# State-space recurrence of a two-layer trunk: scan instructions in a rotating frame, with tables in another tile and the output products at another place on TensorE

## The chip, the cores and the metric

The kernel runs on one core of a Trainium2 chip. The metric is the device time of one execution in microseconds. Engines are named as in the profile: PE is TensorE, DVE is VectorE, ACT is ScalarE, POOL is GpSimd, SP is the queue that issues most DMAs.

## What is computed

A decoder trunk of two layers on 512 tokens of width 1024. Layer 0 projects the normed input once (q, k, v, gate of a retention head group and u of a state-space group), runs retention and the state-space mixer in parallel, joins them in one output projection, and goes through a mixture of 16 experts; layer 1 is dilated attention and a second mixture. The change touches the state-space mixer of layer 0, 32 groups of 16 channels with 64 complex states each:

```python
def s5_mixer(u, a_re, a_im, b_re, b_im, c_re, c_im, d_skip, log_dt, w_glu, b_glu):
    ...
    zr, zi = a_re * dt, a_im * dt
    mag = jnp.exp(zr)
    lam_re, lam_im = mag * jnp.cos(zi), mag * jnp.sin(zi)
    ...
    bu_re = jnp.einsum('blgh,gph->blgp', uf, bb_re)
    bu_im = jnp.einsum('blgh,gph->blgp', uf, bb_im)
    ...
    _, _, xr, xim = lax.associative_scan(combine, (ar, ai, bu_re, bu_im), axis=1)   # x[l] = lam * x[l-1] + bu[l]
    y = (jnp.einsum('blgp,ghp->blgh', xr, c_re.astype(f32))
         - jnp.einsum('blgp,ghp->blgh', xim, c_im.astype(f32))
         + d_skip.astype(f32) * uf)
    g = jax.nn.gelu(y.reshape(B, L, S5_WIDTH))
    return g * jax.nn.sigmoid(g @ w_glu.astype(f32) + b_glu.astype(f32))
```

## The kernel before

Everything is float32. A GEMM (`gemm`) runs as three products of 512 columns for each 128 rows of K (`mm3`, lines 197 to 199), from a high and a low part of each operand; `split_to` (line 194) makes the high part on ACT (a cast) and the low part on DVE (a product row "L194 TENSOR_TENSOR"), into a ring of three R tiles. A projection of 512 outputs takes 8 blocks of K, 4 token blocks and 3 products each: 96 products of `mm3`, in the order of K, and each token block is handed to an evacuation function at the end.

The state-space mixer works on chunks of 8 tokens, 64 of them, and in two halves `hf` of 16 groups. `s5_tables` makes the powers of lambda: `L` (0 to 8) and `M8` (lambda to the 8th, 16th, up to the 64th) by `cmul`, a complex product of six small DVE instructions. `s5_in_tables`, `s5_CL` and `s5_K` make the matrices for PE, on DVE, POOL, ACT and PE together. `s5_conv` computes what a chunk gives to itself, into the PSUM tiles `py`. `s5_in` gives each chunk's contribution X to the state (512 values for each of the real and the imaginary part of a half), `s5_scan` turns X into the states at the chunk ends, and `s5_cross` (line 598) adds C times the state before each chunk into `py`: 256 products of 32 by 63 in a half, followed by GELU on ACT.

`s5_scan` before does the recurrence over 64 chunk values as 8 blocks of 8: seven steps within all blocks, seven across the blocks' last values, seven that spread them. A step is four DVE instructions (lines 519 to 522), so 84 in a half.

`layer0_mix` calls, in this order: the v GEMM, the u GEMM, the tables, `s5_conv` of half 0, `s5_in` of both halves, the q GEMM, `s5_scan` and `s5_cross` of half 0, `s5_conv` of half 1, the k GEMM, `s5_scan` and `s5_cross` of half 1, then the gate GEMM, the GLU GEMM and the retention. `ev_q` and `ev_k` rotate q and k (`rot`: three DVE products, a POOL sum) and transpose them on PE (line 190). A scheduler orders each engine's instructions when the program is built, by program order and by when it expects operands; `tc.issue_after(x)` keeps what follows behind x on that engine. At run time each engine takes its instructions strictly in this order and waits at the first whose operands aren't there.

`growt` is the row tile of the norm weights; before, the next norm's row is loaded into it early on ACT's queue. `M8` shares its place with `srt`, a small table of the router. `m4s` are two work tiles of 1024 values, `spare4` holds `Bb` and `CTc`, tables that are read until `s5_CL` is done.

## Time and profile before

| | us |
|---|---|
| median of 3 runs | 1160.1 (1155.97 to 1160.4) |
| the profiled execution | 1166.1 |
| its span, first to last instruction | 1164.3 |
| PE busy in the span | 1061.4 (91%) |
| DVE busy in the span | 739.4 (64%) |

The profile is of one execution. Starts are counted from the span's beginning. A row's bracket tells how long its engine sat idle before it and which instruction ended that. PE's products are pipelined: two that follow each other start closer together than one of them is long, so steps between starts are used for what a run of them costs. [...]

### The profile page before, as it was taken

How to read it: one execution, taken by the hardware profiler on the slowest of the kernel's cores; microseconds unless marked ns; L12 is line 12 of the kernel's file. 1: busy time of each engine (PE TensorE's matmuls, PEld its weight loads, DVE VectorE, ACT ScalarE, POOL GpSimd, SP SyncE). 2: the span in 40 equal slices, each digit the busy share in tenths (PEclk: the TensorE clock that was granted, in tenths of full speed). 3: DMA queues.
4: the chain of work that ended last, by engine and by line, in shares of the span. 5: the costliest groups of instructions: out<-in, count | busy, mean ns of one | idle time of the engine just before them, and what ended most of it. 6: DMA issues, size and time to landing. Idle time of an engine off the chain costs nothing. (4 is left out here: it accounts for less than half of the span.)

```text
span 1164.3 us, 16088 instructions
## 1 busy us (share of the span) xinstructions
PE 1061.4 (91%) x5951; PEld 772.1 (66%) x5951; DVE 739.4 (64%) x1356; ACT 564.9 (49%) x853; POOL 188.2 (16%) x120
## 2 busy tenths in 40 slices
PE   6989877899789999999979999999978999999994
PEld 5767666787566765666448877877766676566641
DVE  6964957577687866756373264266578786666644
ACT  6333133614466755646352255254446675555634
POOL 3553120000121322111100000000012131211111
PEclk9999988999899999998989999999989999989998
DMA  8243032348398999999953223323439999999963
GB/s 252 74 144 110 36 113 74 110 153 312 107 399 334 383 397 375 388 365 359 334 205 110 90 73 145 109 73 141 191 130 402 347 387 396 384 387 370 367 257 145
DMA packets 84714, 277.39 MB, mean 238 GB/s; under 512 B 23715, under 2 KB 23899, under 8 KB 68369
## 3 DMA queue, kind: packets, MB, share of 16 engines
q1 hardware_dynamic: 72000, 248.31, 56.5%
q0 software_dynamic: 8016, 16.88, 5.8%
q10 hardware_dynamic: 4608, 11.06, 2.5%
q8 instruction: 51, 0.84, 0.3%
q14 instruction: 39, 0.31, 0.1%
HBM read 262.49 MB, written 24.12 MB: 246 GB/s over the span
## 5 line engine op out<-in xcount | busy, mean ns | idle before, releaser
L198 PE MATMUL acc<-R,R 128*128 128x512 f32 x936 | 384.4, 411 | 16.7 <-DVE R L194 15.9
L197 PE MATMUL acc<-R,R 128*128 128x512 f32 x860 | 354.1, 413 | 26.6 <-ACT R L194 16.5
L199 PE MATMUL acc<-R,R 128*128 128x512 f32 x860 | 345.2, 404 | 0.2 <-DVE R L194 0.2
L194 DVE TENSOR_TENSOR R<-F,R 128x1024 fp32r<-128x1024 f32 (+1 forms) x178 | 213.0, 1218 | 148.5 <-ACT R L194 144.3
L194 ACT CAST R<-F 128x1024 fp32r<-128x1024 f32 (+1 forms) x178 | 182.4, 1040 | 187.4 <-PE acc L199 115.4
L198 PEld LDWEIGHTS acc<-R,R 128*128 128x128 f32 x936 | 180.8, 193 | 66.8 <-DVE R L194 28.3
L197 PEld LDWEIGHTS acc<-R,R 128*128 128x128 f32 x860 | 166.1, 193 | 68.9 <-ACT R L194 22.9
L199 PEld LDWEIGHTS acc<-R,R 128*128 128x128 f32 x860 | 166.6, 194 | 36.3 <-DVE R L194 1.8
L1203 POOL DMA_INDIRECT F<-xnd,idx x30 | 51.0, 1700 | 238.0 <-DVE ws L1013 114.0
L1285 PE MATMUL acc<-F,R 128*64 128x512 f32 x304 | 71.2, 595 | 0.0
L194 DVE TENSOR_TENSOR R<-pb,R 128x512 fp32r<-128x512 f32 x84 | 56.7, 686 | 15.2 <-ACT R L194 15.2
L1357 POOL DMA_INDIRECT hd<-m,idx x20 | 36.6, 1832 | 152.1 <-ACT m L1356 130.2
L194 ACT CAST R<-pb 128x512 fp32r<-128x512 f32 x84 | 47.7, 587 | 27.1 <-PE pb L190 21.1
L903 POOL MEMSET R<- 128x1024 f32 x2 | 1.9, 955 | 313.2 <-PE acc L199 313.2
L194 DVE TENSOR_TENSOR R<-R,R 128x1024 fp32r<-128x1024 f32 x40 | 48.2, 1221 | 6.3 <-ACT R L194 5.9
L1285 PEld LDWEIGHTS acc<-F,R 128*64 128x64 f32 x304 | 22.0, 137 | 43.6 <-issue 42.6
L194 ACT CAST R<-R 128x1024 fp32r<-128x1024 f32 x40 | 41.3, 1050 | 13.5 <-PE acc L199 13.3
L197 PE MATMUL acc<-spare,R 128*128 128x512 f32 x116 | 46.0, 397 | 0.0
L199 PE MATMUL acc<-spare,R 128*128 128x512 f32 x116 | 45.9, 395 | 0.0
L190 PE MATMUL pb<-C,F 128*128 128x128 f32 (+1 forms) x296 | 38.3, 265 | 3.4 <-POOL F L478 3.4
L1288 ACT ACTIVATE m2w<-acc 64x512 f32<-64x512 f32 x8 | 4.8, 594 | 69.4 <-PE acc L1285 69.4
L190 PEld LDWEIGHTS pb<-C,F 128*128 128x128 f32 (+1 forms) x296 | 30.0, 142 | 10.9 <-issue 5.6
(379 smaller groups left out, 1464.7 us busy)
## 6 DMA issues: line engine op xcount, KB each, us to landing
F<-in_moe_w_up_dram SPq DMA_DIRECT2D x46, 1024.0 KB, 22.9
F<-in_moe_w_down_dram SPq DMA_DIRECT2D x40, 1024.0 KB, 22.1
F<-in_moe_w_gate_dram SPq DMA_DIRECT2D x38, 1024.0 KB, 22.8
R<-in_moe_w_gate_dram SPq DMA_DIRECT2D x20, 1024.0 KB, 23.6
R<-in_moe_w_down_dram SPq DMA_DIRECT2D x12, 1024.0 KB, 25.0
h<-in_moe_w_down_dram SPq DMA_DIRECT2D x12, 1024.0 KB, 22.2
F<-in_c_w_qkv_dram SPq DMA_DIRECT2D x12, 1024.0 KB, 5.7
F<-in_ab_w_in_dram SPq DMA_DIRECT2D x10, 1024.0 KB, 5.1
```

Source lines behind the costliest of these rows:

```text
L190: PE.transpose(dst, src, ident[:n, :n])
L194: return S.copy(hi, src), eng.tensor_tensor(lo, src, hi.bitcast(F32), op=OP.subtract)
L197: PE.matmul(ps, ah, bh, start=first, stop=False)
L198: PE.matmul(ps, ah, bl, start=False, stop=False)
L199: return PE.matmul(ps, al, bh, start=False, stop=last)
L903: G.memset(q.x0, 0.0)
L1203: rows[e] = G.indirect_dma_start(out=xg[e % 2][0:n], out_offset=None, in_=xnd[:, :], in_offset=bass.IndirectOffsetOnAxis(ap=idx[0:n, e, 0: ...
L1285: m = PE.matmul(ps[LIGHT * i:LIGHT * i + LIGHT], x_[:, 4 * kk + k, :], raw[i][:, k, :], start=kk + k == 0, stop=kk + k == 4, skip_group_ch ...
L1288: silu = S.activation(hs[0:LIGHT], ps[LIGHT:2 * LIGHT], AF.Silu)
L1357: G.indirect_dma_start(out=hd[:, :], out_offset=bass.IndirectOffsetOnAxis(ap=idx[:, e, 1:2], axis=0), in_=y[:, :], in_offset=None, bounds_ ...
```

## The change

The recurrence x[n] = r e^(i a) x[n-1] + b[n] (r and a are the modulus and the angle of lambda to the 8th) is done in a frame that turns by a at each step: with z[n] = e^(-i a n) x[n] it becomes z[n] = r z[n-1] + e^(-i a n) b[n], with a real factor, so the real and the imaginary part can each be done by one scan instruction over 8 rows of 64 values (`tensor_tensor_scan`; the factor is zero at each row's first value). `s5_tables` makes r (`r8`, an exponential on ACT) and the turning factors' powers 0 to 7 and 0, 8, up to 56 (`rot`, nine `cmul` instead of three for `M8`), in `growt`. A new function `s5_rotor` multiplies these out to 64 factors for each state (`E`, six DVE products of 512) and spreads r (`rt`, a copy and a memset); it uses an `m4s` tile and a part of `spare4`. `s5_scan` turns X (four products), scans it (two), and turns it back (four products): 10 instructions and the rotor's 8 for 84. The cross products are kept (`gemm.last`, which `gemm` now notes) behind the last product of the q GEMM (half 0) and of the k GEMM (half 1), the second rotor behind the last rotation of q. `srt` gets a place of its own.

```diff
...
@@ -394,7 +396,8 @@
         V.tensor_scalar(cs, cs, -2.0, 1.0, op0=OP.mult, op1=OP.add)
         L = F[H0][:, 896:1184].rearrange("p (a i q) -> p a i q", a=9, i=2)
         cmt = F[H0][:, 1184:1312].rearrange("p (i a q) -> p i a q", i=2, a=4)
-        M8 = sm.tile([128, 384], F32, bufs=1, tag="M8", name="M8").rearrange("p (m i q) -> p m i q", m=8, i=3)
+
+        r8, rot = growt[:, 544:560], growt[:, 0:544].rearrange("p (n i q) -> p n i q", n=17, i=2)
...
@@ -437,12 +440,21 @@
         V.tensor_tensor(t3[:, 1], Br[:, 0], cib, op=OP.mult)
         V.tensor_tensor(Bb[:, 0], Bb[:, 0], t3[:, 0], op=OP.subtract)
         V.tensor_tensor(Bb[:, 1], Bb[:, 1], t3[:, 1], op=OP.add)
-        N8 = M8[:, :, 0:3:2, :]
-        V.tensor_copy(N8[:, 0], L[:, 8])
-        cmul(N8[:, 1:2], N8[:, 0:1], N8[:, 0], 1)
-        cmul(N8[:, 2:4], N8[:, 0:2], N8[:, 1], 2)
-        cmul(N8[:, 4:8], N8[:, 0:4], N8[:, 3], 4)
-        V.tensor_scalar(M8[:, :, 1, :], M8[:, :, 2, :], -1.0, None, op0=OP.mult)
+        S.activation(r8, zr, AF.Exp, scale=8.0)
+        V.tensor_copy(rot[:, 1, 0, :], cs)
+        V.tensor_copy(rot[:, 1, 1, :], sn)
+        for i in (2, 3):
+            cmul(rot[:, i:i + 1], rot[:, i - 1:i], rot[:, i - 1], 1)
+        cmul(rot[:, 1:2], rot[:, 3:4], rot[:, 3], 1)
+        for g in (0, 9):
+            V.memset(rot[:, g, 0, :], 1.0)
+            V.memset(rot[:, g, 1, :], 0.0)
+            if g:
+                V.tensor_copy(rot[:, 10], rot[:, 8])
+            cmul(rot[:, g + 2:g + 3], rot[:, g + 1:g + 2], rot[:, g + 1], 1)
+            cmul(rot[:, g + 3:g + 5], rot[:, g + 1:g + 3], rot[:, g + 2], 2)
+            n = 3 if g else 4
+            cmul(rot[:, g + 5:g + 5 + n], rot[:, g + 1:g + 1 + n], rot[:, g + 4], n)
         bd = F[H1].rearrange("p (x i q t h) -> p x i q t h", x=2, i=2, q=16, t=2)
         CTd, Bbd = bd[:, 0], bd[:, 1]
         CTc = shaped(spare4[:, 512:1024], [128, 2, 16, 16])
@@ -457,7 +469,7 @@
                 S.copy(CTc[ps_, i], pc[ps_, :, two, :])
                 G.tensor_scalar(CTd[ps_, i, :, two, :], CTc[ps_, i], 1.0 - 2 * i, None, op0=OP.mult)
                 G.tensor_copy(Bbd[ps_, i, :, two, :], Bb[ps_, i])
-        P.update(L=L, M8=M8, Bb=Bb, CTc=CTc, CTd=CTd, Bbd=Bbd)
+        P.update(L=L, rot=rot, r8=r8, Bb=Bb, CTc=CTc, CTd=CTd, Bbd=Bbd)
         return P
 
     def s5_in_tables(P, hf, wslot):
@@ -499,34 +511,36 @@
             S.copy(X[:, i, 8 * hf:8 * hf + 8, :], px)
         return ins
 
-    def s5_scan(P, hf, X):
-        M8 = P["M8"]
+    def s5_rotor(P, hf):
+
         pr = slice(8 * hf, 8 * hf + 8)
-        B = X[:, :, pr, :].rearrange("p r q (b i) -> p r q b i", i=8)
-
-        def swap(v):
-
-            dims = [list(d) for d in v.ap]
-            return bass.AP(tensor=v.tensor, offset=v.offset + dims[1][0], ap=[dims[0], [-dims[1][0], 2]] + dims[2:])
-
-        def step(dst, src, m, n):
-
-            sh = [128, 2, 8, n]
-            mr = M8[:, m, 0, pr][:, None, :, None].to_broadcast(sh)
-            mi = M8[:, m, 1:3, pr][:, :, :, None].to_broadcast(sh)
-            ta = m2([128, 2, 8, 8], "sca")[:, :, :, 0:n]
-            tb = m2([128, 2, 8, 8], "scb")[:, :, :, 0:n]
-            V.tensor_tensor(ta, src, mr, op=OP.mult)
-            V.tensor_tensor(tb, swap(src), mi, op=OP.mult)
-            V.tensor_tensor(dst, dst, ta, op=OP.add)
-            V.tensor_tensor(dst, dst, tb, op=OP.add)
-
-        for i in range(1, 8):
-            step(B[:, :, :, :, i], B[:, :, :, :, i - 1], 0, 8)
-        for b in range(1, 8):
-            step(B[:, :, :, b, 7:8], B[:, :, :, b - 1, 7:8], 7, 1)
-        for i in range(7):
-            step(B[:, :, :, 1:8, i], B[:, :, :, 0:7, 7], i, 7)
+        E = shaped(m4s[hf], [128, 2, 512])
+        rt = shaped(spare4[:, 512 * hf:512 * hf + 512], [128, 8, 64])
+        sh = [128, 8, 8, 8]
+        b_ = [P["rot"][:, 0:8, i, pr].rearrange("p n q -> p q n")[:, :, None, :].to_broadcast(sh) for i in range(2)]
+        a_ = [P["rot"][:, 9:17, i, pr].rearrange("p n q -> p q n")[:, :, :, None].to_broadcast(sh) for i in range(2)]
+        e = [shaped(E[:, i], sh) for i in range(2)]
+        t = shaped(m4s[1 - hf][:, 0:512], sh)
+        for i in range(2):
+            V.tensor_tensor(e[i], a_[0], b_[i], op=OP.mult)
+            V.tensor_tensor(t, a_[1], b_[1 - i], op=OP.mult)
+            V.tensor_tensor(e[i], e[i], t, op=OP.add if i else OP.subtract)
+        V.tensor_copy(rt, P["r8"][:, pr][:, :, None].to_broadcast([128, 8, 64]))
+        V.memset(rt[:, :, 0:1], 0.0)
+        return E, rt.rearrange("p q n -> p (q n)")
+
+    def s5_scan(E, rt, hf, X):
+
+        B = X[:, :, 8 * hf:8 * hf + 8, :].rearrange("p i q c -> p i (q c)")
+        tmp = shaped(m4s[1 - hf], [128, 2, 512])
+        c, s = (E[:, i:i + 1, :].to_broadcast([128, 2, 512]) for i in range(2))
+        for back in range(2):
+            V.tensor_tensor(tmp, B, s, op=OP.mult)
+            V.tensor_tensor(B, B, c, op=OP.mult)
+            for i in range(2):
+                V.tensor_tensor(B[:, i], B[:, i], tmp[:, 1 - i], op=OP.add if i == back else OP.subtract)
+            for i in range(0 if back else 2):
+                V.tensor_tensor_scan(B[:, i], rt, B[:, i], 0.0, op0=OP.mult, op1=OP.add)
 
     def s5_CL(P, hf, CLs):
         L, CTc = P["L"], P["CTc"]
@@ -588,16 +602,17 @@
             ps.append(py)
         return ps
 
-    def s5_cross(hf, ps, CL, X, gT):
+    def s5_cross(hf, ps, CL, X, gT, behind):
         for o in range(2):
             py = ps[o]
             for j in range(8):
                 for i in range(2):
                     for p4 in range(4):
                         q = 4 * o + p4
-                        PE.matmul(py[32 * p4:32 * p4 + 32, j * 64 + 1:(j + 1) * 64], CL[i][:, j, q, :],
-                                  X[:, i, 8 * hf + q, 0:63], start=False, stop=(j == 7 and i == 1),
-                                  skip_group_check=True)
+                        with tc.issue_after(behind.ins):
+                            PE.matmul(py[32 * p4:32 * p4 + 32, j * 64 + 1:(j + 1) * 64], CL[i][:, j, q, :],
+                                      X[:, i, 8 * hf + q, 0:63], start=False, stop=(j == 7 and i == 1),
+                                      skip_group_check=True)
             S.activation(gT[:, 2 * hf + o, :].rearrange("p (c j) -> p j c", j=8),
                          py.rearrange("p (j c) -> p j c", j=8), AF.Gelu_apprx_tanh)
 
@@ -636,8 +651,9 @@
             t2 = m2([128, 4, 2, 64], "rt2")
             V.tensor_tensor(t1, p4, cs[:, c, :][:, None, :].to_broadcast([128, 4, 128]), op=OP.mult)
             for a in range(2):
-                V.tensor_tensor(t2[:, :, a, :], p5[:, :, 1 - a, :],
-                                sn[:, c, 64 * a:64 * a + 64][:, None, :].to_broadcast([128, 4, 64]), op=OP.mult)
+                rot.last = V.tensor_tensor(
+                    t2[:, :, a, :], p5[:, :, 1 - a, :], sn[:, c, 64 * a:64 * a + 64][:, None, :].to_broadcast([128, 4, 64]),
+                    op=OP.mult)
             G.tensor_tensor(t1, t1, t2.rearrange("p h a d -> p h (a d)"), op=OP.add)
             return t1
 
@@ -689,13 +705,16 @@
             last = s5_in(hf, W[hf], U, X)
         K = s5_K(P, 1, CL[1], F[3])
         nc.gpsimd.dma_start(tab, I["tab0"].rearrange("p (a b) -> p a b", a=4))
+        E = s5_rotor(P, 0)
         gemm(xT, win[:, 0:512], 8, ev_q, False, behind=last.ins)
-        s5_scan(P, 0, X)
-        s5_cross(0, py, CL[0], X, gT)
+        s5_scan(*E, 0, X)
+        with tc.issue_after(rot.last.ins):
+            E = s5_rotor(P, 1)
+        s5_cross(0, py, CL[0], X, gT, gemm.last)
         py = s5_conv(1, K, uT)
         gemm(xT, win[:, 512:1024], 8, ev_k, False)
-        s5_scan(P, 1, X)
-        s5_cross(1, py, CL[1], X, gT)
+        s5_scan(*E, 1, X)
+        s5_cross(1, py, CL[1], X, gT, gemm.last)
         R[4:6] = typed((4, 5), F32R)
         ghi, glo = v3(R[4], 4), v3(R[5], 4)
         for o in range(4):
@@ -860,7 +879,7 @@
                             idx=sm.tile([128, NE, 2], I32, bufs=1, name="idx"), ohf=[], xn=[])
         part = {}
         if l == 0:
-            srts.append(sm.tile([128, 208], F32, bufs=1, tag="M8", name="srt"))
+            srts.append(sm.tile([128, 208], F32, bufs=1, name="srt"))
             nc.scalar.dma_start(srts[0][:, 0:86], I["srt"])
         q.srt = srts[0]
```

On PE, the place after the q GEMM. The names: `R_` and `acc` are a GEMM's operands and sums, `m_4`, `m2w` the rotated q, `h` the state-space matrices X, `F_74`/`F_75` the matrices of `s5_CL`, `pb` PSUM tiles. Before, half 0's cross products stand behind 58 of the k GEMM's 96 products:

```order
L198 MATMUL acc<-R_86,R_81 128x512
L199 MATMUL acc<-R_86,R_83 128x512
L197 MATMUL acc<-R_86,R_81 128x512
L598 MATMUL pb<-h,F_74 32x63 [waits DVE_49]
L598 MATMUL pb<-h,F_74 32x63 x3
L598 MATMUL pb<-h,F_75 32x63 x4
```

Now they stand behind q's first two groups of transposes, ahead of the second convolution and of all of the k GEMM:

```order
L199 MATMUL acc<-R_86,R_83 128x512
L190 MATMUL pb<-C,m_4_88 128x128 [waits PE_49,Activation_49,Pool_49]
L190 MATMUL pb<-C,m_4_88 128x128 x3
L190 MATMUL pb<-C,m2w 128x128 [waits PE_49,Activation_49,Pool_49]
L190 MATMUL pb<-C,m2w 128x128 x3
L613 MATMUL pb<-h,F_74 32x63 [waits DVE_49]
L613 MATMUL pb<-h,F_74 32x63 x3
L613 MATMUL pb<-h,F_75 32x63 [waits DVE_49]
```

What moved are the 256 products of each half: half 0's from the middle of the k GEMM to its front, half 1's from three products before the end of the gate GEMM to the end of the k GEMM, between the transposes of k. Between the first convolution and the input products (L497) there stood 8 products of the q GEMM, now 2; the other six stand earlier.

On DVE, the same stretch of the program. Before, the two splits of the k GEMM are followed by the rotations of q (L637, L639), and the first scan comes among and after these:

```order
L194 TENSOR_TENSOR R_84<-F_78,R_84 128x1024 [waits DMAHW1_49,Activation_49]
L194 TENSOR_TENSOR R_85<-F_78,R_85 128x1024 [waits Activation_49]
L637 TENSOR_TENSOR m_4_88<-acc,F_77 128x512 [waits DMASW0_49,PE_49]
L639 TENSOR_TENSOR m_5_89<-acc,F_77 128x4x64 x2
L637 TENSOR_TENSOR m2w<-acc,F_77 128x512 [waits PE_49]
```

Now the whole first scan (the L543 row is the two scan instructions) stands between these splits:

```order
L194 TENSOR_TENSOR R_84<-F_78,R_84 128x1024 [waits DMAHW1_49,Activation_49]
L538 TENSOR_TENSOR m_1_91<-h,m_0_90 128x1024 [waits DMAHW0_49,DMAHW3_49,DVE_49,Activation_49]
L539 TENSOR_TENSOR h<-h,m_0_90 128x2x512 [waits DVE_49]
L541 TENSOR_TENSOR h<-h,m_1_91 128x512 [waits DVE_49]
L541 TENSOR_TENSOR h<-h,m_1_91 128x512
L543 SCALAR_TENSOR_TENSOR h<-spare_108,h 128x512 [waits DVE_49] x2
L538 TENSOR_TENSOR m_1_91<-h,m_0_90 128x1024 [waits DVE_49]
L539 TENSOR_TENSOR h<-h,m_0_90 128x2x512 [waits DVE_49]
L541 TENSOR_TENSOR h<-h,m_1_91 128x512 [waits DVE_49]
L541 TENSOR_TENSOR h<-h,m_1_91 128x512
L194 TENSOR_TENSOR R_85<-F_78,R_85 128x1024 [waits Activation_49]
L652 TENSOR_TENSOR m_4_88<-acc,F_77 128x512 [waits DMASW0_49,PE_49]
L654 TENSOR_TENSOR m_5_89<-acc,F_77 128x4x64 x2
```

The rotations of q follow behind it, then the second rotor, one split, and the second scan.

On DVE, earlier, where the tables are made beside the u GEMM. Before, these rows stand ahead of the split that the u GEMM's third quarter needs (its last row here):

```order
L411 TENSOR_TENSOR M_256<-M_256,h 128x4x16 [waits DVE_49]
L479 TENSOR_TENSOR F_72<-spare_108,h 128x1024
L445 TENSOR_SCALAR M_256<-M_256 128x8x16 [waits DVE_49]
L480 TENSOR_TENSOR m_0_90<-spare_108,h 128x1024
L481 TENSOR_TENSOR F_72<-F_72,m_0_90 128x1024 [waits DVE_49]
L194 TENSOR_TENSOR R_84<-F_79,R_84 128x1024 [waits DMAHW5_49,PE_49,Activation_49]
```

Now more of the tables and a second L492 (the same product as L480) stand ahead of that split:

```order
L492 TENSOR_TENSOR m_0_90<-spare_108,h 128x1024
L414 TENSOR_TENSOR growt<-growt,h 128x16 [waits DVE_49]
L409 TENSOR_TENSOR growt<-growt 128x16 [waits DVE_49]
L493 TENSOR_TENSOR F_72<-F_72,m_0_90 128x1024 [waits DVE_49]
L410 TENSOR_TENSOR h<-growt 128x16 [waits DVE_49]
L411 TENSOR_TENSOR growt<-growt 128x16
L412 TENSOR_TENSOR h<-growt 128x16
L413 TENSOR_TENSOR growt<-growt,h 128x16 [waits DVE_49]
L492 TENSOR_TENSOR m_0_90<-spare_108,h 128x1024
L414 TENSOR_TENSOR growt<-growt,h 128x16 [waits DVE_49]
L409 TENSOR_TENSOR growt<-growt 128x2x16 [waits DVE_49]
L194 TENSOR_TENSOR R_84<-F_79,R_84 128x1024 [waits DMAHW5_49,PE_49,Activation_49]
```

The split moved back behind one 1024-element product and six more small ones than before; another 30 small ones stand between it and the next split.

On ACT the load of the next norm's row into `growt` moved from the start to behind half 0's GELU, the load of `srt` from the gate GEMM to the start, and half 1's GELU ahead of the gate's SiLU. On SP the load for the output projection that goes into `s5_CL`'s tile moved ahead of the load for the gate GEMM's second half. From the middle of the retention on, PE, POOL and SP have the same order as before.

## Rows read from the trace of the kernel before

**Rows 1.** The page, part 1: each engine's busy time, share of the span, instructions.

```profile
PE 1061.4 (91%) x5951; PEld 772.1 (66%) x5951; DVE 739.4 (64%) x1356; ACT 564.9 (49%) x853; POOL 188.2 (16%) x120
```

**Rows 2.** Waits from 100 to 225 us: total us, times, longest us.

```profile
PE pb L598 <- DVE h L522: 12.5, 2, 6.4
...
PE pb L598 <- issue: 4.0, 2, 2.0
```

**Rows 3.** PE's timeline at L598: start, length, instructions, count, idle before.

```profile
148.68 4.70 PE L598 MATMUL pb<-h,F 128*32 128x63 f32 x218 [6.40 <-DVE h L522]
...
155.35 0.75 PE L598 MATMUL pb<-h,F 128*32 128x63 f32 x38 [1.98 <-issue]
...
198.62 4.64 PE L598 MATMUL pb<-h,R 128*32 128x63 f32 x172 [6.07 <-DVE h L522]
...
205.28 1.60 PE L598 MATMUL pb<-h,R 128*32 128x63 f32 x84 [2.02 <-issue]
```

**Rows 4.** Windows: length, busy PE PEld DVE ACT POOL, granted clock, DMA share, GB/s.

```profile
148.68:150.00 1.32, 1.32 (x52) 1.32 (x56) 1.07 (x1) 0.00 (x0) 0.00 (x0) 0.50 0.61 56
...
152.00:153.38 1.38, 1.38 (x98) 1.22 (x87) 0.00 (x0) 1.14 (x1) 0.00 (x0) 1.00 0.72 270
...
198.60:200.00 1.40, 1.38 (x54) 1.38 (x58) 0.00 (x0) 0.63 (x1) 0.00 (x0) 0.50 0.45 26
...
206.90:210.00 3.10, 3.10 (x8) 2.48 (x9) 1.89 (x3) 3.08 (x6) 0.00 (x0) 0.54 0.68 225
...
210.00:215.00 5.00, 5.00 (x23) 4.02 (x22) 1.92 (x3) 3.13 (x4) 0.00 (x0) 1.00 0.19 74
```

**Rows 5.** L519 on DVE: busy time and count in the first scan; two timeline rows.

```profile
123.50:148.70 25.20, 6.64 (x21) 0.92 0.00 1
...
128.20 0.39 DVE L519 TENSOR_TENSOR m<-h,M 128x128 f32<-128x128 f32 x1
...
128.50 0.38 DVE L520 TENSOR_TENSOR m<-h,M 128x128 f32<-128x128 f32 x1
```

**Rows 6.** DVE timeline: two instructions in a row, of 1024 and of 512 elements.

```profile
55.73 2.35 DVE L194 TENSOR_TENSOR R<-F,R 128x1024 fp32r<-128x1024 f32 x2
...
219.14 1.28 DVE L710 TENSOR_TENSOR m2w<-m2w,F 128x512 f32<-128x512 f32 x2
```

**Rows 7.** DVE timeline in the stage of the tables, and PE's wait there.

```profile
36.45 1.21 DVE L194 TENSOR_TENSOR R<-F,R 128x1024 fp32r<-128x1024 f32 x1
...
41.15 2.05 DVE L411 TENSOR_TENSOR M<-M,h 128x32 f32<-128x32 f32 x1
...
53.46 1.22 DVE L194 TENSOR_TENSOR R<-F,R 128x1024 fp32r<-128x1024 f32 x1
...
54.74 0.50 PE L199 MATMUL acc<-R,R 128*128 128x512 f32 x1 [0.18 <-DVE R L194]
```

**Rows 8.** PE timeline before the first convolution, and DVE's last row of `s5_CL`.

```profile
85.03 0.58 PE L564 MATMUL pb<-F,h 128*32 128x224 f32 x8 [1.37 <-DVE F L548]
...
89.47 0.70 PE L586 MATMUL pb<-F,F 128*128 128x512 f32 x1 [2.10 <-POOL F L578]
...
94.97 2.45 DVE L548 SCALAR_TENSOR_TENSOR R<-m,m 64x1024 f32<-64x1024 f32 x2 [1.82 <-POOL m L541]
```

**Rows 9.** ACT, DVE and PE timelines around the end of the q GEMM.

```profile
103.35 0.58 ACT L499 COPY h<-pb 128x512 f32<-128x512 f32 x1 [0.39 <-PE pb L497]
...
105.19 0.58 ACT L499 COPY h<-pb 128x512 f32<-128x512 f32 x1 [0.36 <-PE pb L497]
...
115.03 0.68 DVE L637 TENSOR_TENSOR m<-acc,F 128x512 f32<-128x512 f32 x1
...
117.99 0.60 PE L190 MATMUL pb<-C,m 128*128 128x128 f32 x4
```

**Rows 10.** Windows of the expert stage that follows, columns as in Rows 4.

```profile
220.00:400.00 180.00, 166.13 (x933) 128.20 (x932) 137.03 (x280) 91.67 (x133) 27.78 (x17) 0.95 0.72 269
...
400.00:560.00 160.00, 152.38 (x748) 102.22 (x748) 103.40 (x127) 91.24 (x112) 29.96 (x17) 0.98 1.01 378
```

6 lines of the change are left out of this document (4 added, 2 removed).

## Prediction

> **What bounds the kernel now.** I read the page first: TensorE (PE) is busy for 91% of the span, so only time in which PE stands idle or runs at the lower clock can be won [rows 1]. Next the waits of PE between 100 and 225 us, the stretch in which the changed functions run: its largest wait by far is L598 (the cross products of `s5_cross`) behind DVE L522 (the last line of a scan step), 12.5 us in two waits, and L598 also loses 4.0 us in two gaps marked "issue", in which PE waits for nothing that the profile shows [rows 2]. PE's timeline puts them in place: 6.40 us before the first half's products and 6.07 us before the second's, and a 2 us gap inside each burst [rows 3]. [...] After the second burst the 512-column products of the next GEMM also run slow, 8 in 3.10 us against 23 in 5.00 us at clock 1.00 [rows 4]. So the scan chain on DVE is what PE waits for, twice, and each wait also costs clock. Elsewhere around it PE is dense.
>
> The profiled execution took 1166.1 us (span 1164.3 and 1.8 around it), 6.0 us above the median of the runs, 1160.1. The sum below is a difference within that execution; I carry it to the median unchanged.
>
> **What is taken away.** The old scan is 84 DVE instructions a half, 21 on each of four lines; line L519's 21 alone are busy 6.64 us in the first half, so the four lines about 4 x 6.64 = 26.6 us [rows 5]. All of it goes.
> - The two waits: 12.47 us, if the new scans end before PE asks (checked below).
> - The lower clock in the bursts: the first burst's 218 products take 4.70 us and the second's first 172 take 4.64 us [rows 3]. At 71 a us (98 in 1.38 us) they would take 3.07 and 2.42, so 1.63 + 2.22 = 3.85 us. Bounds: 0 (if something other than the clock sets their pace) to 3.85. I take 3.85, since the same burst shows both rates.
> - The slow start of the following GEMM: 8 products at 5.00/23 = 0.217 us each are 1.74 us instead of 3.10, so 1.36 us; bounds 0 to 1.36.
> - Fillers: the order before has 8 products of the q GEMM between the convolution and the input products (L497), after it 2. Six more thus stand ahead, where PE waits 1.37 us for DVE and 2.10 us for POOL anyway [rows 8]: 6 x 0.217 = 1.30 us; bounds 0 to 1.30.
> - The two "issue" gaps, 4.0 us: the cross products stay the same dense run of small instructions, so I leave them where they are; bounds 0 to 4.0 gained.
>
> About those gaps: the rows show PE waiting 1.98 and 2.02 us with no releaser [rows 3]. [...]
>
> **What is added, and where it lands.**
> - *Tables.* The turning powers take 9 complex products of 6 small DVE instructions where `M8` took 3. By the order, what stands between the split at 36.45 us and the split at 53.46 us that PE waited for at the second GEMM is now one more 1024-element product (it came after that split before) and 6 more small ones. A 1024-element step is 1.13 us (two take 2.35, one 1.22) [rows 6]; a small one steps by 0.1 to 0.15 us. With two copies and an exponential ahead of the first split (0.3 us) that is 1.13 + 0.7 + 0.3 = 2.1 us. PE has no slack there: its fill of products just covers the 53.46 us split now. Bounds: 1.1 (the large product alone) to 3.3 (small ones at the slowest step seen, 0.27 us); a small product can also stand 2.05 us behind POOL [rows 7], but POOL's four operations there block one each, before and after. So -2.1. The other 30 small instructions come after this split and before the next one, which has 5.2 us (24 products at 0.217): cover holds, and nothing is charged.
> - *Radii of half 0.* A 512-element copy and a memset now stand ahead of the DVE products that `s5_CL` hands to PE, on the path that ends PE's 1.37 and 2.10 us waits [rows 8]: 0.60 + 0.1 = 0.7 us (a 512-element step is 0.60: two take 1.28, one 0.68 [rows 6]). Bounds 0 to 1.3. So -0.7.
> - *Turning factors of half 0* (6 products of 512) run where DVE idled, behind `s5_CL`, which ends at 97.4 us (94.97 and 2.45 [rows 8]). Their reads are strided; bounds 0.60 (contiguous) and 1.20 us each (by L519: steps of 0.30 us for 128 strided elements, 2.34 ns each [rows 5]), 3.6 to 7.2 us. Off PE's path by themselves.
> - *Scan 0* now stands on DVE ahead of the rotations of q. The convolution shifts by 2.1 + 0.7, less the fillers, so X is complete at about 107 us (ACT's fourth copy starts at 105.19 now), and its first half at about 105.4 (the second copy starts at 103.35 now [rows 9]). Behind the factors and one 1.13 us split the scan starts at 105.4 to 108.5. It is four 1024-element and four 512-element products, 4 x 1.13 + 4 x 0.60 = 6.9 us, 0.9 us for waits on its own results, and two scan instructions. No row shows a scan. Bounds from rows: 0.60 us (any 512-element product) and 1.20 (the strided rate); I take the upper, as one element hangs on the last. So 9.0 to 10.2 us, and the scan ends at 114.4 to 118.7. Then comes one split (1.13), so q's rotations can start at 115.5 to 119.8. Their data are there at 115.03 now [rows 9], about 116.5 after the shift. The delay is 0 to 3.3 us; PE, whose queue has the transposes of q (117.99 now [rows 9]) ahead of the cross products, stands idle for it. I take 1.5.
> - *Cross 0* then finds its scan done: the rotations, POOL's sum and two groups of transposes all come behind it. *Scan 1* and its factors start after the last rotation (about 124 us), end by about 143, and their products are asked for behind the second convolution and the whole k GEMM; the GEMM alone is 96 x 0.217 = 20.8 us after the end of cross 0 near 128. Over 5 us of slack without the convolution: no charge.
> - *Queues.* ACT's load of the next norm row now waits for DVE's last read of the radii (about 131 us); behind it stands the cast for the last quarter of k, wanted three quarters through the k GEMM, later than that. SP's load for the gate GEMM's second half now stands behind the load that waits for cross 0 (about 128), earlier than its own slot is free. The 43 KB load at the start of ACT's queue is small beside the 1 MB loads. All nothing; if the cover goes, 1 to 2 us each.
>
> [...]
>
> **Sum.** 12.47 + 3.85 + 1.36 + 1.30 - 2.1 - 0.7 - 1.5 = 14.7 us. The profiled execution would take 1151.4, the median 1160.1 - 14.7 = **1145.4**. Best ends together: 12.47 + 3.85 + 1.36 + 1.30 + 4.0 - 1.1 = 21.9; worst ends: 12.47 - 3.3 - 1.3 - 3.3 = 4.6.
>
> **Rivals.**
> 1. *The gaps and the clock all go, the tables hide*: cross products mixed with transposes give PE no dense burst. Gain about 21, time 1139. For it: the second half's products stand between transposes in the new order. Against: 218 products in a row showed the gap at full clock.
> 2. *The costs sit at their upper ends*: DVE is late for the second GEMM and for q's rotations, and the clock gains are small. Gain 5 to 9, time about 1153. For it: a 32-element DVE product took 2.05 us in the stage of the tables [rows 7], and more small ones stand there now.
> 3. *The gain is given back later*: from 400 to 560 us DMA is at share 1.01 [rows 10], and if its stream did not start earlier, the expert stage would end when it does now: 1160. Against: between 220 and 400 us DMA's share is 0.72, and its loads wait for buffers that PE, DVE and ACT free, which all come earlier.
> 4. *Slower: the scan instruction is serial and slow.* Each element needs the one before it, and no row shows such an operation. With s us per scan, q's transposes come 2s - 0.9 us late. The gain is used up at 2s = 17, s = 8.5 us (17 ns an element); at s = 12 PE stands idle for 23 us and the time is 1160 - 16 + 23 = 1167. Against: the slowest DVE rate in this trace is 2.34 ns an element, seven times less than the turning point.
>
> **Chances.** Forecast 0.50 (own range 1140 to 1150), rival 1 0.18, rival 2 0.18, rival 3 0.08, rival 4 0.06. A measurement of this kernel tells about 0.5%, 5.8 us, from no change: faster by more (under 1154.3) is the forecast, rival 1 and most of rival 2, 0.84; same 0.10; slower 0.06. The range takes in both ends of the sum (1138.2 and 1155.5) and a little for the spread of the runs: 1136 to 1156.
>
> **What would show it.** Right: no wait of PE behind the scan's last line, cross products at clock 1.00 directly behind q's transposes; two "issue" gaps of 2 us still there; a wait of about 2 us of PE for a DVE split near 54 us; a wait of 0.5 to 3 us before q's first transposes near 120; scan instructions near 1.2 us; everything after the gate GEMM the same, 15 us earlier. Wrong: a scan instruction of several us, PE idle at q's transposes for over 4 us, or an expert stage that ends at its old time.

## The result, and the profile after

The changed kernel takes **1143.9 us** (median of four runs, 1140.3 to 1145.4) against 1159.5 for the kernel before (1156.0 to 1160.4): a ratio of 0.9866, 95% interval 0.9835 to 0.9898, a gain of 15.6 us. A second comparison, six more runs of it against eleven of before, gave 0.9868 (0.984 to 0.9897). The forecast was 1145.4, from a gain of 14.7.

The profiled execution of the changed kernel took 1145.4 us. Its page, part 1 (busy time, share of the span, instructions; it answers [rows 1]):

```profile
PE 1050.0 (92%) x5951; PEld 762.0 (67%) x5951; DVE 734.0 (64%) x1265; ACT 562.2 (49%) x852; POOL 190.1 (17%) x120
```

VectorE (DVE) issues 91 instructions fewer, but is busy only 5.4 us less: its trace has 44.1 us for the two old scans, and 19.8 for the new ones, 15.3 for their factors and radii and 4.1 more for the tables now. What the change bought is shown by the waits of TensorE (PE) from 100 to 225 us (who waited for whom; total us, times, longest):

```profile
PE pb L190 <- POOL m L657: 3.0, 1, 3.0
PE pb L190 <- POOL m2w L657: 2.3, 3, 1.2
PE acc L197 <- ACT R L194: 1.6, 1, 1.6
PE pb L190 <- ACT F L672: 0.7, 1, 0.7
```

Both kinds of wait of [rows 2] are gone, the 12.5 us behind the scan and the 4.0 us of "issue". The waits for GpSimd's sum in the rotations (POOL L657) and for ACT L672 are 6.0 us together, 4.2 more than the 1.8 that the same places had before. PE's timeline shows the first half's cross products (L613) in their new place (start, length, instruction, count, idle before):

```profile
123.03 0.66 PE L190 MATMUL pb<-C,m 128*128 128x128 f32 x4 [2.97 <-POOL m L657]
124.30 1.11 PE L190 MATMUL pb<-C,m2w 128*128 128x128 f32 x4 [0.61 <-POOL m2w L657]
125.34 2.69 PE L613 MATMUL pb<-h,F 128*32 128x63 f32 x98
127.97 0.66 PE L190 MATMUL pb<-C,m2w 128*128 128x128 f32 x4
128.55 0.85 PE L613 MATMUL pb<-h,F 128*32 128x63 f32 x44
129.34 0.66 PE L190 MATMUL pb<-C,m 128*128 128x128 f32 x4
129.92 1.84 PE L613 MATMUL pb<-h,F 128*32 128x63 f32 x114
```

They come in pieces of 98, 44 and 114 between q's transposes, with no pause among them, where [rows 3] had 218 and 38 around one of 1.98 us. The reason for the 2.97 us in front stands in VectorE's timeline, which shows the factors (L525 to L527), scan 0 (L538 to L543), a weight split (L194) and only then the first of q's rotations (L652):

```profile
102.43 1.10 DVE L525 TENSOR_TENSOR m<-growt 128x512 f32<-128x512 f32 x1
...
107.90 1.22 DVE L194 TENSOR_TENSOR R<-F,R 128x1024 fp32r<-128x1024 f32 x1
109.03 1.22 DVE L538 TENSOR_TENSOR m<-h,m 128x1024 f32<-128x1024 f32 x1
...
113.05 2.33 DVE L543 TENSOR_TENSOR_SCAN h<-spare,h 128x512 f32<-128x512 f32 x2
...
119.15 1.22 DVE L194 TENSOR_TENSOR R<-F,R 128x1024 fp32r<-128x1024 f32 x1
120.28 0.68 DVE L652 TENSOR_TENSOR m<-acc,F 128x512 f32<-128x512 f32 x1
```

The windows answer [rows 4] (busy PE, PEld, DVE, ACT, POOL, then the granted clock as a share of PE's full one, DMA share, GB/s):

```profile
125.34:128.00 2.66, 2.66 (x100) 2.57 (x99) 2.28 (x5) 0.00 (x0) 1.38 (x2) 0.57 0.02 6
129.92:131.70 1.78, 1.78 (x116) 1.69 (x115) 1.78 (x3) 0.50 (x1) 0.00 (x0) 1.00 0.05 9
...
175.00:180.00 5.00, 5.00 (x22) 4.11 (x23) 2.59 (x4) 3.13 (x5) 0.00 (x0) 1.00 0.53 213
```

Behind the 2.97 us wait the first piece runs at a granted clock of 0.57, near the 0.50 that [rows 4] has behind each wait; the following pieces and the gate GEMM run at 1.00.

**Where the time went.** The end of the GLU GEMM (the first scores product starts there) is a good mark, since the order of PE's work behind it is the same. Both kernels were profiled twice, unchanged; PE's timeline gives:

| us | before | before, again | after | after, again |
|---|---|---|---|---|
| end of the u GEMM | 65.3 | 65.7 | 68.4 | 66.9 |
| end of the q GEMM | 118.2 | 118.5 | 120.1 | 116.9 |
| gate GEMM's long run starts | 174.2 | 174.2 | 174.9 | 171.7 |
| end of the GLU GEMM | 220.1 | 219.3 | 208.0 | 204.8 |
| from there to the end of the span | 944.2 | 939.0 | 935.6 | 936.2 |

At the GLU GEMM's end the gain is 12.1 us in the first pair and 14.5 in the second. Note that the two profiles of the changed kernel differ by 3.2 us there, with nothing edited between them. The second pair adds up as follows: waits for the scan −12.4, "issue" −3.3, the cross products themselves −0.9 (11.8 us busy before, 10.9 after), waits at the rotations' transposes +4.2, the tables' stage +1.3, the K stage up to the end of the q GEMM −2.9: −14.0. The 0.5 us left over hide two larger shifts that cancel: between the end of the q GEMM and the mark the 240 GEMM products take 2.4 us less, the transposes and the products of L679 (L663 before) 2.4 more. In the first pair the tables' stage cost 3.1 us, not 1.3, and the K stage gave back 1.2, not 2.9.

### The profile page after: what moved, and what is told of

Read it like the earlier page. It is cut to its first block, busy times and chain, and to the rows that moved or that the text cites. A ratio compares the mean times of both kernels' runs of the same rounds, so it can differ in the third digit from the quotient of the medians.

```text
span 1143.6 us, 15992 instructions
## 1 busy us (share of the span) xinstructions
PE 1050.0 (92%) x5951; PEld 762.0 (67%) x5951; DVE 734.0 (64%) x1265; ACT 562.2 (49%) x852; POOL 190.1 (17%) x120
## 5 line engine op out<-in xcount | busy, mean ns | idle before, releaser
L194 DVE TENSOR_TENSOR R<-F,R 128x1024 fp32r<-128x1024 f32 (+1 forms) x178 | 212.9, 1218 | 138.1 <-ACT R L194 133.1
L194 ACT CAST R<-F 128x1024 fp32r<-128x1024 f32 (+1 forms) x178 | 182.4, 1040 | 180.6 <-PE acc L199 107.7
L198 PEld LDWEIGHTS acc<-R,R 128*128 128x128 f32 x936 | 179.2, 191 | 67.7 <-DVE R L194 28.9
L197 PEld LDWEIGHTS acc<-R,R 128*128 128x128 f32 x860 | 164.2, 191 | 67.7 <-ACT R L194 22.5
L199 PEld LDWEIGHTS acc<-R,R 128*128 128x128 f32 x860 | 164.8, 192 | 37.7 <-DVE R L194 3.3
L194 DVE TENSOR_TENSOR R<-pb,R 128x512 fp32r<-128x512 f32 x84 | 57.3, 702 | 14.6 <-ACT R L194 14.5
L194 ACT CAST R<-pb 128x512 fp32r<-128x512 f32 x84 | 47.5, 586 | 27.4 <-PE pb L190 20.9
L194 DVE TENSOR_TENSOR R<-R,R 128x1024 fp32r<-128x1024 f32 x40 | 48.2, 1221 | 6.4 <-ACT R L194 6.0
L194 ACT CAST R<-R 128x1024 fp32r<-128x1024 f32 x40 | 41.4, 1050 | 13.2 <-PE acc L199 12.1
L190 PE MATMUL pb<-C,F 128*128 128x128 f32 (+1 forms) x296 | 37.5, 261 | 3.4 <-POOL F L490 3.4
L190 PE MATMUL pb<-C,m 128*128 128x128 f32 (+1 forms) x163 | 27.7, 292 | 12.7 <-DVE m L227 9.6
```

Of the source, the lines that this page charges most:

```text
L190: PE.transpose(dst, src, ident[:n, :n])
L194: return S.copy(hi, src), eng.tensor_tensor(lo, src, hi.bitcast(F32), op=OP.subtract)
L197: PE.matmul(ps, ah, bh, start=first, stop=False)
L198: PE.matmul(ps, ah, bl, start=False, stop=False)
L199: return PE.matmul(ps, al, bh, start=False, stop=last)
```

## The experiments

**Both kernels once more.** Nothing edited.

> The changed kernel once more, nothing edited. In the two profiles compared so far the lead over the kernel before is 12.1 us at the end of the GLU GEMM (208 us) and 20.7 us at the end, while the medians differ by 15.6 us. Theory 1 (the last 8.6 us are differences between single executions, since the code behind 208 us is the same in the same order): this profile's time lies 2 us or more from the first one's 1145.4 us or its stretches behind 287 us differ from the first profile's by several us in the same places (287 to 307, 307 to 332, 534 to 607). Theory 2 (they belong to the change): the lead at every place repeats within 1 us. Time expected 1140 to 1145 us.

> The kernel before once more, nothing edited. Theory (what the first pair of profiles shows behind 275 us, 8.6 us, is mostly the clock behind the routers' short pauses, which differs between executions of one kernel): against the first profile of before, this one is shifted by under 0.7 us up to 270 us and by 2 us or more in the stretches 285 to 310, 325 to 335, 530 to 610 or 840 to 870, and the granted clock there differs. Rival (these stretches are the same in each execution of before, and the change itself made them shorter): shifts under 1 us everywhere, the clock in these stretches as in the first profile.

Measured: 1143.7 us (six runs, 1141.6 to 1147.8) for the changed kernel; 1160.1 for the profiled run of the kernel before, and 1160.1 as the median of 17. Up to 285 us the two profiles of before agree within 0.9 us at nearly all places behind the K stage; from the router's stretch on the second pulls ahead, to 6.0 us at the end, 5.2 of them won behind the mark. Windows of the two there (columns as above; the clock is the third number from the end). The profile shown ahead of the prediction has

```profile
288.00:298.00 10.00, 9.74 (x63) 9.52 (x63) 5.24 (x21) 1.48 (x5) 0.29 (x1) 0.66 0.42 114
...
302.00:312.00 10.00, 8.20 (x47) 5.93 (x47) 4.30 (x15) 3.12 (x5) 1.43 (x1) 0.66 0.02 6
```

and the second one has

```profile
288.00:298.00 10.00, 6.45 (x60) 6.04 (x59) 8.70 (x27) 4.33 (x7) 0.29 (x1) 1.00 0.38 94
...
302.00:312.00 10.00, 7.40 (x52) 5.15 (x51) 7.70 (x13) 6.81 (x8) 5.09 (x3) 0.97 0.41 131
```

The first row of each is the same place, 0.9 us apart, at a clock of 0.66 in one execution and 1.00 in the other. From the transposes of the router (L190, behind idle times of 0.35 and 0.56 us in the one and 0.36 and 0.56 in the other) to the next product that PE waits for, the first took 9.66 us and the second 6.40. By the second row the two are 4.5 us apart, so these are not the same products. PE stands idle here for 0.26 to 4.98 us at a time (first profile, 285 to 304 us), and behind the same short pauses the clock fell in one execution and not in the other. Theory 1 holds by the two profiles of before: of the 8.6 us by which the first pair of profiles drew further apart behind 208 us, 5.2 are a difference between two executions of one kernel. The two profiles of the changed kernel agree within 0.6 us behind the mark; what differs between them lies ahead of it. Over all thirteen profiles of this study the time from the GLU GEMM's end to the end of the span lies between 934.5 and 944.2 us (936.1, 940.9, 936.7, 935.4, 936.8, 938.0, 943.3, 940.9 and 934.5 us in the nine experiments with edits, in the order e4, e3, e5, e6, e8, e1, c1, e2, c3), and PE's order behind that mark is the same. An edit worth 1 to 3 us can hardly be seen in the median. At the mark a single profile does not show it either, as the 3.2 us above tell; the wait that the edit was meant for does.

**The cross products set free (e1).** The new recurrence, without the rule that holds the cross products back:

```diff
-                        with tc.issue_after(behind.ins):
+                        if True:
                             PE.matmul(py[32 * p4:32 * p4 + 32, j * 64 + 1:(j + 1) * 64], CL[i][:, j, q, :],
...
```

> The new recurrence with its cross products free: nothing holds them behind the last product of the q or the k GEMM, so that the planner puts cross 0 between the two halves of s5_in, near 105 us. Theory (scan 0 ends near 119 us whatever stands on TensorE, so placement is what hides it): TensorE waits about 12 to 15 us for the last line of the scan in front of cross 0, q's GEMM ends as much later, and most of the change's 16 us is lost: 1152 to 1160 us. The wait is followed by half clock and by a pause of about 2 us without a named wait inside the dense stretch, as in the kernel before. Rival (the scan moves forward with its reader, since VectorE would take it earlier): a wait of under 5 us, 1143 to 1148 us.

Measured: 1159.3 us (one run), the GLU GEMM's end at 219.5: nothing is left of the gain. PE's timeline:

```profile
118.29 5.08 PE L613 MATMUL pb<-h,F 128*32 128x63 f32 x248 [11.97 <-DVE h L541]
124.98 0.32 PE L613 MATMUL pb<-h,F 128*32 128x63 f32 x8 [1.60 <-issue]
```

Scan 0 did not move forward for its reader; PE waited 11.97 us for its last line, and the dense run of 248 products has its "issue" pause again. The theory holds for the order that the planner makes of it: cross 0 now stands ahead of the q GEMM, 30 us earlier than in the kernel before, and there the faster scan is worth nothing. That is not the reader's old place; e3 below has it near there.

**The placement without the new recurrence (e2).** The step-by-step scan of before, cross 0 moved behind the k GEMM:

```diff
...
-        s5_cross(0, py, CL[0], X, gT)
-        py = s5_conv(1, K, uT)
-        gemm(xT, win[:, 512:1024], 8, ev_k, False)
+        py, py0 = s5_conv(1, K, uT), py
+        gemm(xT, win[:, 512:1024], 8, ev_k, False, end=lambda: s5_cross(0, py0, CL[0], X, gT, gemm.last))
...
```

> The kernel before with its step-by-step recurrence, but cross 0 held behind the last product of the k GEMM (ahead of k's transposes) and the second convolution ahead of the k GEMM; cross 1 stays behind the gate GEMM. Theory (scan 0's wait is a matter of placement, scan 1's is not: VectorE stood idle for 10.88 us between the two scans, so scan 1 moves forward with the k GEMM, but it still ends 30 us after k's rotations begin): no wait in front of cross 0, scan 1 ends 6 to 8 us earlier, the wait in front of cross 1 stays near 6 us, time 6 to 9 us under the kernel before's. Rival 1 (VectorE is the bound between the two scans): the wait in front of cross 1 grows to 12 us or more and the time is the kernel before's within 2 us. Rival 2 (placement is the whole change): 14 us or more under the kernel before's. As to the pause of 2.0 us without a named wait in the dense cross stretch: if it comes from the wait or the half clock ahead of it, it is gone at cross 0 here; if from the dense run of small products, it stays at both.

Measured: 1157.1 us, ratio 0.9966 (0.9941 to 0.9991), so 3.1 us, half of the least that I expected. PE's timeline:

```profile
155.89 2.72 PE L601 MATMUL pb<-h,F 128*32 128x63 f32 x180
160.30 1.29 PE L601 MATMUL pb<-h,F 128*32 128x63 f32 x76 [1.69 <-issue]
...
193.47 4.19 PE L601 MATMUL pb<-h,R 128*32 128x63 f32 x178 [6.31 <-DVE h L524]
200.08 2.32 PE L601 MATMUL pb<-h,R 128*32 128x63 f32 x78 [2.42 <-issue]
```

Cross 0 has no wait, as expected, and cross 1 kept one of 6.31 us. What I had not seen is that the long scan 0 now stands on VectorE ahead of a weight split that PE needs: the k GEMM waits 3.08 us for it. So this placement alone gives 3 us, the recurrence alone, in the planner's order, under 1, both together 12 to 15 at the mark. In this run the "issue" pause came with neither a wait nor the lower clock right ahead of it: cross 0 here follows a GEMM without a wait, 180 products take 2.72 us at a granted clock of 1.00 (156 to 160 us), and the pause comes all the same.

**Scan 0 behind q's rotations (e3).**

```diff
-        s5_scan(*E, 0, X)
         with tc.issue_after(rot.last.ins):
+            s5_scan(*E, 0, X)
             E = s5_rotor(P, 1)
```

with cross 0 and the second convolution in the middle of the k GEMM.

> Scan 0 stands behind the last of q's rotations on VectorE, and cross 0 and the second convolution in the middle of the k GEMM (behind its first 48 products). Theory (the 3.1 us that q's first transposes wait longer than before come from scan 0, 10.1 us, and a weight split standing ahead of q's rotations): the wait of 2.97 us at q's transposes falls to under 0.7 us, scan 0 runs from about 123 to 134 us, cross 0 waits 0 to 2 us for it, scan 1 ends near 150 to 158 us, before cross 1 at 161 us, and the time is 1 to 3 us under the changed kernel's. Rival (the wait only moves): cross 0 waits for scan 0 by 3 us or more, or cross 1 waits for scan 1, and the time is the changed kernel's within 1 us.

Measured: 1145.6 us, ratio 0.9887 (0.985 to 0.9923). At the mark, where its first 120 us ran like the first profile of after, it is 2.7 us ahead (205.3 against 208.0): the wait at q's transposes is gone, cross 0 waits 0.67 us for the scan, and one "issue" pause came back in its dense run:

```profile
139.93 3.38 PE L615 MATMUL pb<-h,F 128*32 128x63 f32 x226
144.29 0.42 PE L615 MATMUL pb<-h,F 128*32 128x63 f32 x14 [0.98 <-issue]
```

The time does not follow: behind the mark this execution took 940.9 us. The mechanism is shown, a gain in time is not. The run says one thing more: with cross 0 in the middle of the k GEMM, behind 48 of its 96 products where the kernel before had 58, the new scan is in time but for 0.67 us. For half 0 it is the short scan that ends the wait; its place behind the q GEMM is not needed for that.

**The rotor's table in another layout (e4).**

```diff
-rot = growt[:, 0:544].rearrange("p (n i q) -> p n i q", n=17, i=2)
+rot = growt[:, 0:544].rearrange("p (i q n) -> p n i q", n=17, i=2)
```

> The power table is stored with the power as its last dimension, so that the rotor's four broadcast products read it in steps of 4 bytes, not 128. Theory (the step of 128 bytes makes such a product 1.01 us, the two contiguous ones take 0.60): the four products fall to about 0.6 us each, the rotor by 1.6 us, and since scan 0, the split and q's rotations stand behind it, the wait at q's transposes falls by about 1.6 us, and so does the time. Rival (the broadcast, with a step of 0, or four dimensions cost the time): the four products stay at 0.9 to 1.0 us and the time is the changed kernel's within 0.5 us.

Measured: 1145.6 us, ratio 0.9894 (0.9854 to 0.9934). VectorE's timeline of that run has the product that took 1.10 us at

```profile
99.51 0.69 DVE L525 TENSOR_TENSOR m<-growt 128x512 f32<-128x512 f32 x1
100.12 0.68 DVE L526 TENSOR_TENSOR m<-growt 128x512 f32<-128x512 f32 x1
```

and the wait at q's first transposes fell from 2.93 or 2.97 to 1.56 us. The step of 128 bytes, not the broadcast, made these products 1.1 us long (1.08 to 1.13 in after, 0.68 to 0.69 here). At the mark the run is 1.1 us ahead of the faster profile of after (203.7 against 204.8), less than two executions of after differ; the median shows nothing of it. The 1.4 us at the wait are shown, a gain in time is not.

**The powers behind the CL tables (e5)**, on top of e3: the two small power tables are issued behind the last line of `s5_CL`.

> As the run with scan 0 behind q's rotations, and the two power tables of the rotor (some sixty small VectorE products) are issued behind the last of the CL tables instead of in the u GEMM. Theory (they delay the splits and the CL tables that PE waits for): the wait of 1.32 us at the third quarter of the u GEMM falls to about 0.2 us and the wait of 3.10 us at the first K products to at most 2 us, so 1 to 3 us less than that run. [...]

Measured: 1148.4 us, ratio 0.9906 (0.9879 to 0.9934). The theory's two waits are gone, and a longer one came. ScalarE's timeline:

```profile
105.80 1.07 ACT L515 COPY h<-pb 128x512 f32<-128x512 f32 x2 [5.49 <-DVE growt L416]
```

The powers' scratch lies in the tile that becomes X. Moved back, they hold up the copies that write X, and PE waits 4.9 us for these. The early place of the tables is paid for with 2.8 us against e3 (the u GEMM ends at 65.6 here and at 68.4 there) and saves more: e5's mark, 208.7, lies 3.4 us behind e3's.

**The radii's copy behind the CL tables (e8).**

```diff
-        V.tensor_copy(rt, P["r8"][:, pr][:, :, None].to_broadcast([128, 8, 64]))
+        with tc.issue_after(s5_CL.last.ins):
+            V.tensor_copy(rt, P["r8"][:, pr][:, :, None].to_broadcast([128, 8, 64]))
```

> The copy that spreads the radii of half 0 (512 elements) is issued behind the last of the CL tables; in the changed kernel it stands ahead of the first CL product and took 3.90 us in one profile and 2.16 us in another. Theory (this copy, not the small power products, is what the first K products wait for): no wait of over 0.5 us at the first K products (3.10 us in one profile, none in the other, but the K products come 2 to 4 us earlier than in either), K's end near 97 to 100 us against 102.6 and 99.4, and rotor 0 starts no later than before. Rival (GpSimd's half of the tables is late anyway): the first K products start where they start in the faster of the two profiles (81.5 us) and everything behind them is within 1 us of it.

The copy (L528) stood ahead of what PE's 3.1 us wait at the first K products was for. That wait is in the first profile of the changed kernel only. VectorE and GpSimd, first profile:

```profile
75.86 3.90 DVE L528 COPY spare<-growt 128x512 f32<-128x512 f32 x1
```

```profile
74.93 2.80 POOL L555 TENSOR_TENSOR m<-spare,h 128x1024 f32<-128x1024 f32 x1
77.68 1.80 POOL L570 MEMSET F<- 128x2048 f32 x1
```

and in the second, where the memset came later:

```profile
74.37 2.16 DVE L528 COPY spare<-growt 128x512 f32<-128x512 f32 x1
```

```profile
73.44 2.80 POOL L555 TENSOR_TENSOR m<-spare,h 128x1024 f32<-128x1024 f32 x1
77.77 1.81 POOL L570 MEMSET F<- 128x2048 f32 x1 [1.53 <-PE pb L190]
```

The copy ends 0.28 and 0.29 us after GpSimd's running stretch does, at 79.48 and at 76.24. Moved behind the tables, it takes 0.43 us (here at 100.58, and in the run with three edits, below, at 99.41, where GpSimd is idle from 96.90 to 105.30). Measured for e8: the wait of 3.1 us is gone and the next one is 0.41, 1144.8 us (one run), the mark at 206.2. The gain was given back at once: six products of the q GEMM went behind the convolution again, which then waits 2.10 us for GpSimd, as in [rows 8], and starts at a lower clock. Windows of e8 and of after from each convolution's start, 0.68 and 1.00:

```profile
92.60:98.00 5.40, 5.40 (x13) 3.21 (x14) 3.62 (x3) 0.00 (x0) 4.17 (x2) 0.68 0.26 101
```

```profile
94.50:98.00 3.50, 3.50 (x12) 2.17 (x13) 3.45 (x3) 0.31 (x1) 1.89 (x2) 1.00 0.00 0
```

The convolution takes 9.9 us at the one and 8.2 at the other.

**The routing table's load late (e6)**

```diff
-            nc.scalar.dma_start(srts[0][:, 0:86], I["srt"])
+            with tc.issue_after(s5_cross.gelu.ins):
+                nc.scalar.dma_start(srts[0][:, 0:86], I["srt"])
```

> The load of the routing table (srt), which in the changed kernel stands at the start of ScalarE's queue since its tile is no longer shared with the powers, is issued behind cross 1's last Gelu. Theory (the load at the start changed the planner's times and with them ScalarE's order, in which a weight cast went behind two sums of squares): ScalarE's order at the start is that of the kernel before, the wait of 2.2 to 2.6 us for the second weight quarter's split near 16.7 us falls below 1 us, and the u GEMM's first products come 1.5 to 2.5 us earlier. Rival (the x chunks land later, as they share the queues with the load): the order is that of before, the wait stays near 2 us.

Measured: 1141.9 us (one run), the mark at 204.7. ScalarE's order at the start is that of before, and PE's first wait there is back to

```profile
15.20 0.80 PE L198 MATMUL acc<-R,R 128*128 128x512 f32 x1 [0.84 <-DVE R L194]
```

against 2.20 in after. Against the faster profile of after that product starts 0.9 us earlier (16.13 there), and by 56 us nearly all of it is lost: the u GEMM's third quarter starts at 56.12, against 56.34, and waits 1.30 us for VectorE's split behind the tables, however early the GEMM starts. So the start and the tables share one bill, the tables' 1.3 us.

**Three edits, and two (c1, c3).** c1 is e4, e6 and e8 together; c3 is e4 and e6.

> Three edits of the changed kernel together: the power table with the power as its last dimension, the radii's copy of half 0 behind the CL tables, the load of the routing table behind cross 1. Theory (each gives back what the changed kernel pays): 1.6 us at q's transposes, 2 to 3 us at the K products, 2 us at the start, so the GLU GEMM ends 5 to 6.5 us earlier than 204 to 208 us, and the time is 1137 to 1139 us, unless the half clock behind the routers' short pauses takes 2 to 4 us of it. Rival (DMA-bound expert stages take back what comes before them): the lead at 210 us is 5 us, but under 2 us at 400 us, and the time is 1142 to 1144 us.

> Two edits of the changed kernel together: the power table with the power as its last dimension and the load of the routing table behind cross 1; the radii's copy stays where the changed kernel has it. Theory (the copy moved away gave its gain back, since the first convolution then waits 2.1 us for GpSimd and runs at half clock, while the two other edits keep theirs): the wait at q's transposes is under 1.7 us, the GLU GEMM ends 1.4 to 3 us earlier than in the faster profile of the changed kernel, time 1140 to 1143 us. Rival (the gain of 1 to 3 us is lost in the half clock behind the routers' pauses, as in the run with three edits): the lead at 210 us is there, the time 1143 to 1149 us.

Measured: c1 1148.7 us, ratio 0.9893 (0.9868 to 0.9919), mark at 204.5; the wait at q's transposes is gone but the convolution has its 2.10 us and a clock of 0.54 (91.5 to 95 us), and behind the mark this execution took 943.3 us. c3 1142.3 us, ratio 0.9856 (0.9819 to 0.9893), mark at 203.5, the earliest of all. c3's mark is 1.3 us ahead of the faster profile of after, within what two executions of one kernel differ, and its interval covers that of the changed kernel: in time the two are the same.

**Where the "issue" pauses sit.** Nothing edited; this is read from the traces of all thirteen profiles. In the whole of them PE has nine idle stretches of over 0.25 us that are put down to "issue", all in the cross products. Counted in PE's records from the start (products, weight loads and its sequencer's own), each stands right behind record 1473, 1985 or 2753. These are 512 and 768 apart, multiples of 256, while the number of cross products that had gone before varies from 172 to 248. Each trace also has 51 packets of 16384 bytes in queue q8, of the kind "instruction" on the page, about one for each 256 of PE's 12,000 records. One of them lands next to each pause:

| run | behind record | packet has landed, us | products go on, us | between |
|---|---|---|---|---|
| before | 1985 | 153.98 | 155.35 | 1.37 |
| before | 2753 | 203.86 | 205.28 | 1.42 |
| before, again | 1985 | 154.06 | 155.39 | 1.33 |
| before, again | 2753 | 203.92 | 205.33 | 1.41 |
| e1 | 1473 | 123.48 | 124.98 | 1.50 |
| e2 | 1985 | 158.88 | 160.30 | 1.42 |
| e2 | 2753 | 198.59 | 200.08 | 1.49 |
| e3 | 1985 | 142.88 | 144.29 | 1.41 |
| e5 | 1985 | 146.31 | 147.71 | 1.40 |

In the changed kernel cross 0 passes records 1473 and 1729. The packet ahead of the second lands at 128.21 us, PE gets there at 130.45, 2.24 us later (2.27 in its second profile), and there is no pause. At every other such place of the thirteen profiles the packet was there 2.2 us or more ahead, but for one of 1.27 in e1. So PE stands still there until 1.33 to 1.50 us after its packet has landed, and in the changed kernel, with transposes between the pieces, the packet is there in time. It is a reading of times, nine of nine, without an edit made for it; why a packet starts 0.7 to 3.2 us after PE has passed the place 256 records before was not tested.

## Why the prediction was right, step by step

- *The two waits, 12.47 us*: gone, as forecast; 12.4 in the second pair. Scan 1 ends at 146.6 us, cross 1 starts at 163.2: the slack of over 5 us is 16.
- *Half clock in the bursts, 3.85 us*: mis-sized. Its pace of 71 a us is the window at 152.00 of [rows 4]. The cross products were busy 11.6 us before and 10.7 after in the first pair, 0.9 less. Cross 0 saved nothing (5.4 both): behind the new stall in front of it its first 98 products ran at clock 0.57. The many short pieces of cross 1 take 5.3 us. The stall does not put them there in each execution: behind 1.56 us the first 16 of these products took 0.65 us in e4, and all 98 took 1.62 in c3.
- *The slow start of the following GEMM, 1.36 us*: gone, the gate GEMM behind cross 1 runs at clock 1.00. But it belonged to one execution: in the second profile of before the products from 206.9 to 210.0 us already ran at 1.00, where [rows 4] has 0.54.
- *The "issue" gaps, 0*: wrong by their whole size, 4.0 us in the first pair and 3.3 in the second. I reasoned that the products stay one dense run; the order shown ahead of the prediction already cut them into pieces. The nine pauses, of 0.98 to 2.42 us, stand at steps of 256 records and end 1.3 to 1.5 us after a packet of 16384 bytes has landed, so I read that packet as what they wait for. In the new order it is there in time, 2.24 us ahead in the first profile.
- *Fillers, 1.30 us*: right in direction, and rather too small. In e8, where they went back, the convolution waits 0.98 us longer and takes 1.7 us more.
- *Tables, −2.1 us*: −3.1 in the first pair and −1.3 in the second, on either side of the forecast; the first wait at the third quarter is 1.3 us instead of 0.18. The late start of the u GEMM, 1.0 to 1.5 us, which I had called nothing, is part of the same bill (e6).
- *Radii, −0.7 us*: the place was right, the size was not. The copy took 2.16 and 3.90 us, over the upper bound of 1.3, since I priced a copy like a product that runs alone. PE's wait of 3.1 us behind it came in one of the two executions. The copy ended 0.28 and 0.29 us after GpSimd's work in the two, and took 0.43 us with GpSimd idle (c1).
- *q's transposes, −1.5 us within 0 to 3.3*: −3.1, the upper end. Scan 0 ran 10.1 us as worked out (9.0 to 10.2), a scan instruction 1.16 us (1.20 taken), but the factors ended at 107.9 and the scan began at 109.0, behind the range of 105.4 to 108.5, since the K stage was later.
- *Rivals*: the first (gaps go) came true by half, the second (upper ends) by half, and the two cancelled. The third did not happen: the expert stage ended as much earlier as it began. The fourth fell with 1.16 us for a scan instruction.

So the two main waits, 12.5 us, were right by their mechanism. That the total is right to 1 us is luck: two misses of opposite sign cancel, 4 us too little for the gaps, and 4 to 5 too much for the clock of the bursts (3.0) and the stall at q's transposes (1.6).

## What to carry to other kernels

A faster producer pays only if its reader also stands late enough, and a later reader only if the producer is short enough not to hold up other work on its engine; here each alone gave 0 to 3 us of 16, the faster scan alone because the planner then put its reader 30 us earlier. Of a new helper instruction, ask what runs on the other engines beside it, not only how many elements it has: the radii's copy took 0.43 us with GpSimd idle and 2.16 and 3.90 beside its work. An edit worth 1 to 3 us in a kernel like this is read from the wait that it was meant to end; the median and a mark in a single profile vary by as much between two executions.

## What the runs showed of the hardware that I had not expected

- The 512-element fp32 copy on VectorE took 0.43 us with GpSimd idle (c1) and 2.16 and 3.90 us beside GpSimd's work, ending 0.29 and 0.28 us after it. The product just ahead of it (L493, 1024 elements) took 3.25 us beside a GpSimd product and ended 1.09 us after that one; with GpSimd idle such products took 1.21 to 1.23 (before, 49.80 to 53.55 us).
- A four-dimensional product of 512 elements took 1.08 to 1.13 us with a read step of 128 bytes (after) and 0.68 to 0.69 with one of 4 bytes (e4), broadcast in both.
- In the cross products PE stood still nine times in thirteen profiles, for 0.98 to 2.42 us, each time at a step of 256 of its records and until 1.33 to 1.50 us after a 16 KiB packet of the kind "instruction" had landed; the profile puts such a pause down to "issue".
- After the same short idle times, 0.35 or 0.36 and 0.56 us, PE's clock fell in one execution and not in another of the same kernel (0.66 and 1.00 over the same ten us); behind the GLU GEMM these two took 944.2 and 939.0 us.
